# The planner's price of long scalar_tensor_tensor operations, raised from n/960 to n/760

## The chip, the cores and the metric

The kernel runs on one core of one Trainium2 chip. The time is the device time of one execution in microseconds; lower is better. Engines are named as in the profile: PE is TensorE's matrix multiply, PEld its weight loads, DVE is VectorE, ACT is ScalarE, POOL is GpSimd and SP is SyncE, which issues most of the DMAs.

## The reference

The reference is a two-layer encoder trunk on x of shape 1 x 512 x 1024 in float32. Each layer applies four sub-layers, every one with an RMS norm before and after it and a residual addition:

```python
for l in range(DEPTH):                         # DEPTH = 2
    h = swiglu(rms_norm(x, norm_pre[l, 0]), ffn1_gate[l], ffn1_up[l], ffn1_down[l])
    x = x + 0.5 * rms_norm(h, norm_post[l, 0])
    h = parallel_head_groups(rms_norm(x, norm_pre[l, 1]), ...)   # 4 retention heads, 4 gated DeltaNet heads
    x = x + rms_norm(h, norm_post[l, 1])
    h = memory_cross_attention(rms_norm(x, norm_pre[l, 2]), rms_norm(mem, mem_norm[l]), ...)
    x = x + rms_norm(h, norm_post[l, 2])
    h = swiglu(rms_norm(x, norm_pre[l, 3]), ffn2_gate[l], ffn2_up[l], ffn2_down[l])
    x = x + 0.5 * rms_norm(h, norm_post[l, 3])
```

Two lines of it matter here. The norm is `y = x * rsqrt(mean(x * x) + eps) * w`, and the gated DeltaNet group passes its 12 blocks of 128 columns (four heads each of q, k and v) through a centred depthwise convolution of five taps, followed by silu.

## The kernel before

**A planner orders the instructions.** The program is written as threads (Python generators) that yield one operation at a time. `Sched.run` keeps a clock for each engine, asks for each waiting operation when its operands are ready, and emits operations one after another. The emitted order is the order in which each engine executes; the chip then waits on semaphores where data is not there yet. The times of the planner are used for nothing else: a price changes no instruction, only who goes first.

An operation's length is what `cost` returns. When an operation reads what another wrote, the planner adds `SAME` (0.12 us, same engine) or `OTHER` (0.23 us, another engine). Among the operations that wait for an engine, the planner takes the one of the lowest priority number among those that can start no more than `WAIT` later than the earliest one:

```python
SAME, OTHER = 0.12, 0.23
WAIT = {"PE": 0.25, "ACT": 0.3, "DVE": 0.4, "POOL": 0.2, "SP": 0.0}
...
th = min((c for c in cands if c[0] <= t0 + WAIT[e]), key=lambda c: (pr(c[1]), c[0]))[1]
```

A thread shows its next operation only once its present one has been emitted.

**The work.** Every float32 matrix product is done as three products of rounded parts: an operand is split into a high part H (a copy on ACT) and a low part L (a subtraction on DVE), and `mm3` issues H·H, H·L and L·H. The weights come in blocks of 1 MB, named `raw`, loaded by SP into two buffers (`Stream.loader`), and are split by one thread, `Stream.cutter`, into `wts` tiles: an ACT copy and a DVE subtraction of 128x1024. The cutter's priority is 0, 1, 30 or 60, the higher the more split pieces lie ready. The thread `stream` (priority 50) issues the dense matmuls in a fixed order.

**Where the re-priced operations stand.** `stt` is the helper for `scalar_tensor_tensor`, (a op scalar) op b on DVE. Four places issue it on 256 elements or more:

- `chain`, one thread for each of the four row tiles t of x in every transition between sub-layers: twice (a half of 512 each) `x = hw * rsqrt + x`, and twice `tmp = x * rsqrt * wpre`. Between them stand sums of squares on ACT and a rsqrt of small operations, on POOL for most tiles and on DVE for tile 3 (`POST_DVE`, `PRE_DVE`). The priorities of the tiles are `PRIO = (-1, -1, 13, -1)`. Each `tmp` half starts a thread `feat`: four transposes on PE, a copy to uH on ACT, a subtraction to uL on DVE.
- `early.conv.one`: four in a row on `cv`, one for each tap beside the middle one, for each of 12 blocks in each layer.
- `prepare`: eight on `T` of 896 elements, background work in the first sub-layer.

Around a transition, `out_proj` issues the last products of a sub-layer, and `first_group` the first ones of the next: four column blocks on the first 256 rows (which needs the features of tiles 0 and 1), then the same on the other 256 (tiles 2 and 3). In the mixed sub-layer, `ret_head` loads T, q, k and v of a retention head by SP from DRAM, where `side` has put them, and multiplies k by q on PE (`ps<-q,k`); `inverse` and `scan` are the DeltaNet group's chains.

All instructions carry one line number, L235, since the planner's `emit` issues them all.

## Time and profile before

| | us |
|---|---|
| runs of the kernel (median; lowest to highest of 3) | 2445.86 (2445.59 to 2447.47) |
| the profiled execution: its own time | 2445.77 |
| its span, first to last instruction | 2444.0 |
| PE busy in the span | 2399.7 (98%) |
| DVE busy | 1686.7 (69%) |
| ACT busy | 1122.4 (46%) |
| POOL busy | 203.4 (8%) |

The profile is one execution of the program. Its stages are read by windows of time: a transition between sub-layers takes some 40 us of the span (365 to 405 is the first), the gated feed-forward sub-layers some 300, the mixed sub-layer some 300 (layer 0: 405 to 685; layer 1: 1610 to 1880). "Granted clock" (PEclk) is the share of full speed that TensorE was given in a stretch. A matmul's end is modelled, so its start is the safer number.

### The profile page before, as it was taken

The numbers are of one execution on the slowest core, as the hardware profiler recorded it, in microseconds if no ns is written. First come the engines' busy times: TensorE is split into PE (matmuls) and PEld (weight loads), VectorE is DVE, ScalarE is ACT, GpSimd is POOL, SyncE is SP. The second block draws the span as 40 slices with busy tenths as digits, with TensorE's granted clock in tenths as the row PEclk, the third lists the DMA queues.
The fourth block names the chain that finished last, engine by engine and source line by source line (L and its number), as shares of the span: only waits on it lengthen the run. The fifth ranks groups of instructions, "written<-read, shape, count | busy, mean of one in ns | idle before, by whom it ended". The sixth has DMA issues, their size and how long they took to land. (4 is left out here: it accounts for less than half of the span.)

```text
span 2444.0 us, 37654 instructions
## 1 busy us (share of the span) xinstructions
PE 2399.7 (98%) x15206; PEld 2128.4 (87%) x15206; DVE 1686.7 (69%) x2660; ACT 1122.4 (46%) x1886; POOL 203.4 (8%) x584
## 2 busy tenths in 40 slices
PE   8999999999999999999999999999999999999998
PEld 7889888886989889998889998888788898899987
DVE  5588637867776568886388885486877665788852
ACT  4524525742345544555245553366324454455631
POOL 1000001221020020001010000114010200100011
PEclk9999999999999999999999999999999999999999
DMA  6622522355334322334213334225553243133330
GB/s 204 202 95 82 177 86 96 99 175 159 99 121 153 109 86 70 114 108 176 86 35 104 106 120 160 81 93 145 163 153 132 89 164 104 35 104 104 127 141 35
DMA packets 231204, 286.83 MB, mean 117 GB/s; under 512 B 29630, under 2 KB 190966, under 8 KB 231030
## 3 DMA queue, kind: packets, MB, share of 16 engines
q1 hardware_dynamic: 229878, 280.23, 35.6%
q10 hardware_dynamic: 1152, 4.19, 0.4%
q8 instruction: 119, 1.95, 0.3%
q14 instruction: 55, 0.45, 0.1%
HBM read 255.00 MB, written 29.39 MB: 116 GB/s over the span
## 5 line engine op out<-in xcount | busy, mean ns | idle before, releaser
L235 PE MATMUL ps<-uH,wts 128*128 128x256 f32 (+1 forms) x4064 | 973.1, 325 | 2.5 <-ACT sg L235 2.0
L235 PEld LDWEIGHTS ps<-uH,wts 128*128 128x128 f32 x4064 | 690.3, 189 | 63.6 <-ACT sg L235 2.2
L235 PE MATMUL ps<-uL,wts 128*128 128x256 f32 (+1 forms) x2032 | 655.9, 323 | 0.6 <-DVE uL L235 0.6
L235 DVE TENSOR_TENSOR wts<-raw,wts 128x1024 fp32r<-128x1024 f32 (+1 forms) x363 | 408.5, 1134 | 141.9 <-ACT wts L235 139.3
L235 ACT ACTIVATE wts<-raw 128x1024 fp32r<-128x1024 f32 (+1 forms) x363 | 354.5, 983 | 202.8 <-PE ps L235 115.4
L235 PEld LDWEIGHTS ps<-uL,wts 128*128 128x128 f32 x2032 | 386.8, 190 | 30.8 <-DVE uL L235 1.5
L235 PE MATMUL ps<-wts,uH 128*128 128x512 f32 x1152 | 356.8, 391 | 0.0
L235 PEld LDWEIGHTS ps<-wts,uH 128*128 128x128 f32 x1152 | 214.9, 188 | 43.6
L235 PE MATMUL ps<-wts,uL 128*128 128x512 f32 x576 | 224.6, 390 | 0.0
L235 ACT ACTIVATE sg<-ps 128x256 f32<-128x256 f32 (+1 forms) x208 | 98.0, 473 | 273.1 <-PE ps L235 272.8
L235 DVE TENSOR_TENSOR wts<-T,wts 128x1024 fp32r<-128x1024 f32 x120 | 147.0, 1225 | 51.3 <-ACT wts L235 50.7
L235 ACT ACTIVATE wts<-T 128x1024 fp32r<-128x1024 f32 x120 | 126.9, 1057 | 62.8 <-DVE T L235 62.8
L235 PEld LDWEIGHTS ps<-wts,uL 128*128 128x128 f32 x576 | 108.2, 188 | 22.8
L235 DVE TENSOR_TENSOR uL<-h,uH 128x512 fp32r<-128x512 f32 x76 | 51.2, 689 | 107.5 <-ACT uH L235 107.4
L235 POOL TENSOR_SCALAR sm<-sm 128x1 f32<-128x1 f32 (+1 forms) x165 | 39.2, 238 | 836.8 <-ACT junk L235 812.1
L235 ACT ACTIVATE uH<-h 128x512 fp32r<-128x512 f32 x76 | 46.3, 626 | 132.0 <-PE ps L235 126.9
L235 ACT ACTIVATE junk<-ps 128x512 bf16<-128x512 f32 (+1 forms) x96 | 47.0, 490 | 113.6 <-PE ps L235 99.2
L235 POOL TENSOR_SCALAR wpost<-wpost 128x1024 f32<-128x1024 f32 x4 | 20.3, 5087 | 925.7 <-DMA wpost<-in_norm_post_dram 701.0
L235 PE MATMUL ps<-s3H,wts 128*128 128x256 f32 x480 | 94.6, 281 | 0.0
L235 PE MATMUL ps<-s2H,wts 128*128 128x256 f32 x480 | 94.6, 281 | 0.0
L235 PE MATMUL ps<-s1H,wts 128*128 128x256 f32 x480 | 94.6, 281 | 0.0
L235 DVE TENSOR_TENSOR sg<-ps,sg 128x512 f32<-128x512 f32 x120 | 79.9, 685 | 16.0 <-ACT sg L235 15.9
(340 smaller groups left out, 4324.4 us busy)
## 6 DMA issues: line engine op xcount, KB each, us to landing
raw<-in_ffn_up_dram SPq DMA_DIRECT2D x44, 1024.0 KB, 5.2
raw<-in_ffn_down_dram SPq DMA_DIRECT2D x44, 1024.0 KB, 4.9
raw<-in_ffn_gate_dram SPq DMA_DIRECT2D x43, 1024.0 KB, 5.2
raw<-in_w_in_dram SPq DMA_DIRECT2D x32, 1024.0 KB, 6.1
raw<-in_w_out_dram SPq DMA_DIRECT2D x8, 1024.0 KB, 5.7
raw<-in_xattn_q_dram SPq DMA_DIRECT2D x8, 1024.0 KB, 5.1
raw<-in_xattn_k_dram SPq DMA_DIRECT2D x8, 1024.0 KB, 5.0
raw<-in_xattn_v_dram SPq DMA_DIRECT2D x8, 1024.0 KB, 4.9
```

The source lines that it names most:

```text
L235: fn(*a, **kw)
```

## The change

In `cost`, DVE's `scalar_tensor_tensor` of 256 elements or more is priced with n/760 in place of n/960. For 512 elements in SBUF the price goes from 0.07 + 512/960 = 0.603 us to 0.07 + 512/760 = 0.744 us, for 896 from 1.003 to 1.249. No instruction is added, removed or altered; the planner may emit them in another order.

```diff
     if kind == "DVE":
         if name in ("tensor_copy", "tensor_scalar", "memset") and not psum:
             return 0.07 + n / 1920
-        return (0.13 if psum else 0.07) + n / 960
+        return (0.13 if psum else 0.07) + n / (760 if name == "scalar_tensor_tensor" and n >= 256 else 960)
```

## The prediction

> **What bounds the kernel now.** First the page's head: span and busy shares.

> ```profile
> span 2444.0 us, 37654 instructions
> PE 2399.7 (98%) x15206; PEld 2128.4 (87%) x15206; DVE 1686.7 (69%) x2660; ACT 1122.4 (46%) x1886; POOL 203.4 (8%) x584
> ```

> TensorE is the bound; the change touches no matmul. What an order can win or lose is PE's idle 2444.0 − 2399.7 = 44.3 us. The windows by stage say where that lies (columns: stretch, its length, busy time and count of PE, PEld, DVE, ACT, POOL, then granted clock, DMA share, GB/s).

> ```profile
> 0.00:20.00 20.00, 9.22 (x46) 8.36 (x47) 11.55 (x30) 10.88 (x16) 5.68 (x22) 1.00 0.73 239
> 20.00:365.00 345.00, 341.85 (x1840) 296.19 (x1838) 223.27 (x289) 137.20 (x172) 7.14 (x22) 1.00 0.42 136
> 365.00:405.00 40.00, 38.71 (x263) 34.91 (x262) 29.60 (x74) 19.80 (x42) 11.40 (x44) 1.00 0.29 99
> 405.00:520.00 115.00, 114.81 (x584) 94.01 (x583) 82.70 (x152) 78.05 (x157) 27.62 (x61) 1.00 0.43 122
> 520.00:685.00 165.00, 158.43 (x1184) 132.51 (x1183) 126.61 (x279) 61.05 (x134) 8.30 (x8) 0.98 0.43 138
> ...
> 1720.00:1880.00 160.00, 153.35 (x1161) 129.10 (x1161) 119.46 (x269) 54.09 (x124) 8.30 (x8) 0.97 0.42 129
> ...
> 2070.00:2110.00 40.00, 38.71 (x249) 34.25 (x248) 29.54 (x73) 17.44 (x39) 12.35 (x48) 1.00 0.07 20
> ...
> 2437.00:2444.00 7.00, 0.00 (x0) 0.00 (x0) 3.62 (x14) 0.69 (x2) 0.00 (x0) 0.61 0.28 105
> ```

> Start and end hold 10.8 + 7.0 us, the first sub-layer 3.2, the two retention stretches 6.6 + 6.6 and each of seven transitions about 1.3. The waits of PE name the releasers (total, times, longest).

> ```profile
> PE ps L235 <- DVE tmp L235: 17.1, 9, 8.5
> PE ps L235 <- DMA k<-qkd: 11.8, 2, 6.1
> ...
> PE ps L235 <- DVE uL L235: 1.9, 8, 0.6
> ```

> The 8.5 is the start, before any product. Of DVE's work only `tmp` and `uL` in the transitions keep PE waiting, 17.1 − 8.5 + 1.9 = 10.5 us in all.

> **The change, part by part.** The re-priced operations are these groups:

> ```profile
> L235 DVE SCALAR_TENSOR_TENSOR cv<-xp,cwT,cv 128x512 f32<-128x512 f32 x96 | 74.6, 788 | 11.3 <-ACT cv L235 9.0
> L235 DVE SCALAR_TENSOR_TENSOR x<-tmp,sm,x 128x512 f32<-128x512 f32 x64 | 45.8, 749 | 54.7 <-POOL sm L235 54.4
> L235 DVE SCALAR_TENSOR_TENSOR tmp<-x,sm,wpre 128x512 f32<-128x512 f32 x64 | 45.4, 750 | 7.7 <-POOL sm L235 6.3 <-DMA wpre<-in_norm_pre_dram 0.4 <-POOL sel L235 0.3
> L235 DVE SCALAR_TENSOR_TENSOR T<-crel,lg,T 128x896 f32<-128x896 f32 x8 | 9.2, 1150 | 0.2
> ```

> The plan counts (96 + 64 + 64) × 0.141 + 8 × 0.246 = 33.5 us more on its DVE clock; the chip's own durations stay. So the direct term is 0, and all turns on order.

> *Is the new price nearer?* A record of 0.75 us looks like 0.744. But a plan's price is the distance to the next operation, and its latency is price plus 0.12 or 0.23. The timeline has both:

> ```profile
> 2080.74 0.75 DVE L235 SCALAR_TENSOR_TENSOR x<-tmp,sm,x 128x512 f32<-128x512 f32 x1 [1.47 <-POOL sm L235]
> 2081.58 0.63 ACT L235 ACTIVATE junk<-x 128x512 bf16<-128x512 f32 x1 [0.90 <-DVE x L235]
> ...
> 2099.29 1.42 DVE L235 SCALAR_TENSOR_TENSOR tmp<-x,sm,wpre 128x512 f32<-128x512 f32 x2
> ```
> ```profile
> 430.95 3.10 DVE L235 SCALAR_TENSOR_TENSOR cv<-xp,cwT,cv 128x512 f32<-128x512 f32 x4
> ```

> Two independent ones take 1.42, so the second starts 1.42 − 0.75 = 0.67 after the first: the old price is 0.07 short, the new one 0.07 long. To ACT it is 2081.58 − 2080.74 = 0.84: the old plan says 0.603 + 0.23 = 0.83, the new 0.97. A tap that waits for the tap before starts (3.10 − 0.75) / 3 = 0.78 later: old 0.72, new 0.86. The error changes sign more than size, so I expect no general gain from a truer plan.

> [...]

> *Transitions (seven alike).* Rows of the last one before the final sub-layer's body:

> ```profile
> 2078.78 1.27 PE L235 MATMUL ps<-ident,tmp 128*128 128x128 f32 x8
> 2079.39 0.42 PEld L235 LDWEIGHTS ps<-ident,tmp 128*128 128x128 f32 x4 [0.25 <-issue]
> ...
> 2084.63 1.05 ACT L235 ACTIVATE wts<-raw 128x1024 fp32r<-128x1024 f32 x1
> ...
> 2089.03 0.75 DVE L235 SCALAR_TENSOR_TENSOR x<-tmp,sm,x 128x512 f32<-128x512 f32 x1 [1.14 <-POOL sm L235]
> 2089.69 1.28 DVE L235 TENSOR_TENSOR uL<-ps,uH 128x512 fp32r<-128x512 f32 x2
> ...
> 2090.43 0.19 PEld L235 LDWEIGHTS ps<-uL,wHx 128*128 128x128 f32 x1 [0.49 <-DVE uL L235]
> ...
> 2096.18 1.22 DVE L235 TENSOR_TENSOR wts<-raw,wts 128x1024 fp32r<-128x1024 f32 x1
> ...
> 2101.61 1.41 DVE L235 SCALAR_TENSOR_TENSOR tmp<-x,sm,wpre 128x512 f32<-128x512 f32 x2 [0.90 <-POOL sm L235]
> ...
> 2102.42 1.38 PE L235 MATMUL ps<-ident,tmp 128*128 128x128 f32 x8 [0.88 <-DVE tmp L235]
> ```

> (a) Tiles 0 and 1: eight transposes stand together, with 0.25 us lost between the fours, since the second `tmp` half is late. In the plan four transposes take 4 × 2 × 128/2400 = 0.43 and the second half comes 0.603 after the first: a wait of 0.18, under PE's allowance of 0.25, so the transposes stay together. With 0.744 the wait is 0.32, over it, unless PE came to the first four more than 0.07 late. Then a matmul group goes between and fills the hole. PE's steps are groups of about 0.64 in the plan, so the first four come up to 0.39 late; on time within 0.07 they are in about half of the 14 cases (0.32 of 0.64). Gain 7 × 0.2 = 1.4 us (the quarter, less what the later uH costs); ends 0 and 14 × 0.25 = 3.5.

> (b) The start of `first_group`: PE waits 0.49 for uL, which stands behind `x` of tile 2. The new price makes tiles 0 and 1 later in the plan, so uL stays behind `x`. I take 0. A loss is possible if something slips in ahead of uL (third rival); the best is the whole wait, 7 × 0.49 = 3.4.

> (c) The last `tmp`: PE idles 0.88 because DVE idles 0.90 for POOL's small operations, which are not re-priced. With the POOL chain unhurried the 7 × 0.88 = 6.2 us stay. The cover is gone if DVE's order ahead of that chain changes; tile 2's second `x` comes behind tile 3's chain, whose gaps (0.12 in the plan) are under DVE's allowance of 0.4 by either price, so I take 0.

> *The convolutions.* In 405 to 520 the plan's DVE gets 48 × 0.141 = 6.8 us heavier, against 115 − 82.7 = 32.3 free on the chip; PE is busy 114.8 of 115. The plan may hold the end of this stretch up to 6.8 later against PE. What hides it is that the following chains start from matmuls of the stream. 0 for the stretch itself.

> *Retention.* The largest single stalls are here:

> ```profile
> 555.65 0.38 SPq L235 DMA_DIRECT2D raw<-in_w_in_dram  x1
> 556.09 0.57 SPq L235 DMA_DIRECT2D q<-qkd  x1
> ...
> 563.30 6.04 PE L235 MATMUL ps<-q,k 128*128 128x512 f32 x8 [5.76 <-DMA k<-qkd]
> ```
> ```profile
> 583.02 3.59 PE L235 MATMUL ps<-q,k 128*128 128x512 f32 x8
> ```
> ```profile
> 556.00:566.00 10.00, 4.24 (x11) 2.12 (x10) 9.31 (x23) 4.23 (x5) 0.00 (x0) 0.76 0.65 195
> 566.00:576.00 10.00, 10.00 (x39) 7.10 (x38) 7.59 (x16) 1.06 (x1) 0.00 (x0) 0.90 0.57 180
> ```

> q's load is issued behind a 1 MB weight load; PE stands 5.76 us, the granted clock falls (0.76, then 0.90), and the eight products take 6.04 us where the next head's take 3.59: 5.76 + 2.45 = 8.2 us. Both layers do it (11.8 us in two waits), so the fault is in how the plan prices DMAs and the queue, not in an stt. I take 0; ends −8.2 (gone in one layer) and +5.4 (one more load of 1.05 MB ahead, at the window's 195 GB/s) a layer.

> [...]

> *The rest.* `T` in `prepare`, the initial `tmp` and the final `x` have no rival work whose place matters: 0, hidden by PE's 341.9 of 345 us in the first sub-layer; uncovered, 8 × 0.246 = 2 us.

> **Sum.** −1.4 against the profiled execution's 2445.77 gives 2444.4; the median of the runs is 0.09 above it, hence 2444.5 us.

> **Rivals.**
> 1. *A retention stall goes* (faster). If the re-planned end of the convolutions puts q ahead of the weight load in one layer: 2445.8 − 8.2 = 2437.6; in both 2429. For it: 6.8 us of shift in the plan just ahead. Against: both layers stall alike though they differ in surroundings.
> 2. *The new price is the true one.* Then the waits for `tmp` and `uL` shrink: 10.5 less the 6.2 that POOL makes, 2445.8 − 4.3 = 2441.5, still within 0.2%. Against it stands the 0.67.
> 3. *A weight split ahead of uL* (slower). A split's ACT copy is done from 2084.63 on, and its DVE half waits until 2096.18 for a plan gap over 0.4. The re-pricing makes uL later in the plan by 0.14 and more; where the gap behind tile 2's `x` passes 0.4, the 1.22 us split goes in at 2089.69, and PE waits 1.13 more (what the split holds DVE), seven times 7.9: 2444.4 + 7.9 = 2452.3. Against: in the present plan no gap there is wide enough, and tile 2's second `x`, of better priority than the split, may take the place for 0.67.
> 4. *A later q* (slower): one more load ahead, 2444.4 + 5.4 = 2449.8 for one layer, 2455.2 for both. It decides as soon as a split of the weights is emitted ahead of the rotary products in DVE's queue, since its end lets SP issue that load. For it: DVE is busy 9.31 of the 10 us in which PE stands, so the order there is tight. Against: no price in that stretch is changed.
> 5. *Nothing moves*: the order stays where it counts, 2445.9.

> **How the numbers follow.** About 0.2% (4.9 us) is what a measurement of this kernel can tell from no change. My forecast with 5 and 2 takes 0.52 (0.36, 0.08, 0.08), all "same"; rival 1 0.19, and small gains that add up past 4.9 us 0.02; rival 3 0.12; rival 4 0.15, the larger since a shift of up to 6.8 us in the plan can move q either way and the stall is already there. Faster 0.21, same 0.52, slower 0.27. The range runs from one stall gone, with a little more, 2436.5, to rival 4 in both layers, 2455. The likeliest case alone spans 2441 to 2448.

> **What would show it.** Right: PE busy again 98%; in the transitions some pairs of four transposes parted by dense products; the 0.88 us wait for the last `tmp` still seven times; PE's wait for `k<-qkd` still two of about 6 us. Wrong: that wait gone or above 8 us; a `wts` subtraction between `x` of tile 2 and uL with PE's wait for uL near 1.6; PE waiting behind `cv`; a new idle stretch where the mixed sub-layer's output projection starts, from the DeltaNet chain being emitted later.

## The result and the profile after

The change makes the kernel 0.8% slower: 2465.18 us (median of 4 runs, 2461.08 to 2470.85) against 2445.73 (4 runs, 2443.38 to 2447.47), a ratio of 1.0082 with a 95% interval of 1.0059 to 1.0105. The forecast was 2444.5 and the range ended at 2455. The profiled execution of the changed kernel is its lowest, 2461.08 us with a span of 2459.3, so the profile accounts for 15.3 us. The other three, 2463.21, 2467.15 and 2470.85, have mean granted clocks of 0.994, 0.992 and 0.992 against its 0.995; what such a clock costs is found below. One run each of two kernels below (2644 us, the price on the transitions alone; 2979 us, both together) had a mean granted clock of 0.85 and 0.75 and is left out of the ratios.

The head of the page after, and the windows by stage that answer to those of before (stretch, length, busy time and count of PE, PEld, DVE, ACT, POOL, granted clock, DMA share, GB/s):

```profile
span 2459.3 us, 37627 instructions
PE 2401.3 (98%) x15206; PEld 2127.7 (87%) x15206; DVE 1692.5 (69%) x2660; ACT 1123.2 (46%) x1888; POOL 203.8 (8%) x584
```
```profile
20.00:365.00 345.00, 341.02 (x1844) 295.09 (x1843) 223.85 (x291) 141.03 (x178) 7.78 (x23) 1.00 0.42 136
365.00:405.00 40.00, 38.24 (x268) 35.09 (x267) 30.48 (x73) 20.02 (x39) 11.20 (x43) 1.00 0.31 106
405.00:520.00 115.00, 106.44 (x529) 85.11 (x529) 78.02 (x143) 71.68 (x151) 28.28 (x61) 0.99 0.41 115
520.00:685.00 165.00, 162.33 (x1191) 136.64 (x1190) 126.36 (x280) 60.19 (x134) 9.20 (x8) 0.97 0.42 135
```

The convolution stretch, 405 to 520, had PE busy 114.81 of 115 us before and has it busy 106.44 after: 8.6 us of idle time where there was 0.2. The retention stretch has less idle time than before (2.7 us against 6.6). Nothing else moves much. A finer cut of the first stretch:

```profile
405.00:425.00 20.00, 18.38 (x90) 13.26 (x89) 11.87 (x41) 7.00 (x14) 0.00 (x0) 1.00 0.24 79
425.00:445.00 20.00, 17.45 (x88) 14.06 (x88) 18.82 (x33) 17.29 (x46) 4.27 (x3) 1.00 0.09 27
445.00:465.00 20.00, 20.00 (x100) 16.78 (x101) 16.96 (x21) 16.47 (x38) 1.99 (x1) 1.00 0.52 139
465.00:490.00 25.00, 20.61 (x103) 15.83 (x103) 19.75 (x38) 19.47 (x32) 6.24 (x16) 0.93 0.36 102
```

The waits of PE (total, times, longest) say what is late:

```profile
PE ps L235 <- ACT wts L235: 12.1, 7, 1.7
PE ps L235 <- DVE tmp L235: 11.6, 5, 8.6
PE ps L235 <- DVE gl L235: 9.1, 6, 2.5
PE ps L235 <- DMA k<-qkd: 5.4, 2, 2.9
PE ps L235 <- ACT kT L235: 3.0, 2, 1.5
```

`gl` and `kT` are new. They are operands of the key transposes and of the decay products, both in the convolution stretch. Three of these waits in the timeline (start, length, engine, operation, idle time before it and its releaser):

```profile
424.05 0.39 PE L235 MATMUL ps<-uH,wts 128*128 128x512 f32 x1
425.28 0.63 ACT L235 ACTIVATE kT<-cv 128x512 f32<-128x512 f32 x1
425.96 0.66 PE L235 MATMUL ps<-ident,kT 128*128 128x128 f32 x4 [1.52 <-ACT kT L235]
...
442.95 0.40 PE L235 MATMUL ps<-uH,wts 128*128 128x512 f32 x1
444.73 0.15 DVE L235 COPY gl<-ps 128x4 f32<-128x4 f32 x1
444.94 0.50 PE L235 MATMUL ps<-grow,sel 128*128 128x512 f32 x1 [1.59 <-DVE gl L235]
...
472.38 0.15 DVE L235 COPY gl<-ps 128x4 f32<-128x4 f32 x1
472.59 0.50 PE L235 MATMUL ps<-grow,sel 128*128 128x512 f32 x1 [2.53 <-DVE gl L235]
```

Read them so: the stream's dense matmul at 442.95 is followed by a decay product whose operand DVE writes only at 444.73. PE idles for 1.59 us, and whatever comes later in the planner's order, dense matmuls of the stream among it, starts behind that product.

**Two stretches of each layer.** Three landmarks are easy to find: the first `ps<-ident,tmp` transpose of the transition into the mixed sub-layer (370.10 us before, 368.59 after), the first `ps<-q,k` product (563.30, 569.76) and the first product of the output projection, `ps<-wts,hsH` (675.29, 683.96). The differences of these starts are the first stretch (transposes to q k, with the convolutions) and the second (q k to output projection, with the DeltaNet inverse). In us, layer 0 / layer 1:

| | first stretch | second stretch | all the rest |
|---|---|---|---|
| before | 193.2 / 193.6 | 112.0 / 112.0 | 1833.2 |
| after | 201.2 / 202.6 | 114.2 / 111.0 | 1830.3 |

So 8.0 + 9.0 us are lost in the first stretches, 1.2 in the second ones, and 2.9 are gained elsewhere: 15.3. The rest scatters between 1828 and 1837 us over the kernels below (n/700 apart, which has 1843), so little can be read from its 2.9.

### The profile page after: what moved, and what is told of

It is laid out like the page before. It is cut to its first block, busy times and chain, and to the rows that moved or that the text cites. A ratio compares the mean times of both kernels' runs of the same rounds, so it can differ in the third digit from the quotient of the medians.

```text
span 2459.3 us, 37627 instructions
## 1 busy us (share of the span) xinstructions
PE 2401.3 (98%) x15206; PEld 2127.7 (87%) x15206; DVE 1692.5 (69%) x2660; ACT 1123.2 (46%) x1888; POOL 203.8 (8%) x584
## 5 line engine op out<-in xcount | busy, mean ns | idle before, releaser
L235 PE MATMUL ps<-uH,wts 128*128 128x256 f32 (+1 forms) x4064 | 973.1, 324 | 2.9 <-ACT sg L235 2.0
L235 PEld LDWEIGHTS ps<-uH,wts 128*128 128x128 f32 x4064 | 689.5, 188 | 64.3 <-ACT sg L235 2.2
L235 PE MATMUL ps<-uL,wts 128*128 128x256 f32 (+1 forms) x2032 | 655.0, 322 | 0.2
L235 DVE TENSOR_TENSOR wts<-raw,wts 128x1024 fp32r<-128x1024 f32 (+1 forms) x363 | 408.6, 1132 | 164.2 <-ACT wts L235 151.7
L235 ACT ACTIVATE wts<-raw 128x1024 fp32r<-128x1024 f32 (+1 forms) x363 | 355.1, 983 | 213.4 <-PE ps L235 140.1
L235 PEld LDWEIGHTS ps<-uL,wts 128*128 128x128 f32 x2032 | 386.3, 190 | 31.2 <-issue 1.9
L235 PE MATMUL ps<-wts,uH 128*128 128x512 f32 x1152 | 360.0, 394 | 0.0
L235 PEld LDWEIGHTS ps<-wts,uH 128*128 128x128 f32 x1152 | 215.4, 189 | 43.0
L235 PE MATMUL ps<-wts,uL 128*128 128x512 f32 x576 | 225.1, 391 | 0.0
L235 ACT ACTIVATE sg<-ps 128x256 f32<-128x256 f32 (+1 forms) x208 | 98.0, 473 | 268.9 <-PE ps L235 268.7
L235 DVE TENSOR_TENSOR wts<-T,wts 128x1024 fp32r<-128x1024 f32 x120 | 147.0, 1225 | 49.5 <-ACT wts L235 48.6
L235 ACT ACTIVATE wts<-T 128x1024 fp32r<-128x1024 f32 x120 | 126.9, 1058 | 66.6 <-DVE T L235 66.6
L235 PEld LDWEIGHTS ps<-wts,uL 128*128 128x128 f32 x576 | 108.7, 189 | 22.9
L235 DVE TENSOR_TENSOR uL<-h,uH 128x512 fp32r<-128x512 f32 x76 | 51.4, 691 | 103.8 <-ACT uH L235 103.8
L235 POOL TENSOR_SCALAR sm<-sm 128x1 f32<-128x1 f32 (+1 forms) x165 | 39.2, 238 | 851.9 <-ACT junk L235 826.9
L235 ACT ACTIVATE uH<-h 128x512 fp32r<-128x512 f32 x76 | 46.2, 626 | 126.9 <-PE ps L235 122.6
L235 ACT ACTIVATE junk<-ps 128x512 bf16<-128x512 f32 (+1 forms) x96 | 47.2, 491 | 120.4 <-PE ps L235 106.2
L235 POOL TENSOR_SCALAR wpost<-wpost 128x1024 f32<-128x1024 f32 x4 | 19.4, 4854 | 928.6 <-DMA wpost<-in_norm_post_dram 703.4
L235 PE MATMUL ps<-s1H,wts 128*128 128x256 f32 x480 | 94.0, 280 | 0.0
L235 PE MATMUL ps<-s2H,wts 128*128 128x256 f32 x480 | 94.0, 280 | 0.0
L235 PE MATMUL ps<-s3H,wts 128*128 128x256 f32 x480 | 94.0, 280 | 0.0
L235 DVE TENSOR_TENSOR wLx<-raw,wHx 128x1024 fp32r<-128x1024 f32 x45 | 54.3, 1222 | 51.2 <-ACT wHx L235 51.2
```

The lines of the kernel that those rows point to most:

```text
L235: fn(*a, **kw)
```

## The experiments

Two theories stood at the beginning. In the plan as well as in the trace, the changed kernel lets the eight matmuls of the gates go ahead of the convolution's one transpose (`cw`) at the start of the mixed sub-layer, where the kernel before has them the other way about. *Theory A*: this swap is the loss. *Theory B*: the higher price of the convolution's four products spoils the order of the convolution stretch.

### Swap and price, one at a time

Four kernels make a square. The first gives the changed kernel the old place of the transpose, by a priority:

```diff
-        work = [(self.gates(l, ep, ring), 6, "gates"), (conv(), 7, "conv"), ...
+        work = [(self.gates(l, ep, ring), 6, "gates"), (conv(), 5.5, "conv"), ...
```

> The changed kernel, with the convolution thread's priority 5.5 in place of 7, so that its one transpose of the tap weights goes ahead of the eight gate matmuls at the start of the mixed sub-layer, as it does in the kernel before. Theory A (the loss is that order: the gate matmuls go first and the convolutions start late): the PE waits for kT, kqv and gl in the 40 us behind it go and some 8 us a layer come back, 2446 to 2451 us, with what the transitions lost (0.8 us in two of them) left over. Theory B (the convolutions' higher price makes the order inside the stretch worse, wherever it starts): no more than a third comes back, 2459 us or more.

Measured: 2462.4 us (2458.21 to 2465.61), ratio to the kernel before 1.0070 (1.0056 to 1.0085).

The second gives the kernel before, at the old price, the new place: the transpose waits for the gates' matmuls.

```diff
         def conv():
             cw = self.early_in[0]
+            yield self.has("abmm")
```

> The kernel before, old price, with one line that holds the convolution thread until the eight gate matmuls are emitted. Theory A: it pays the loss without any new price, 5 to 9 us a layer, 2456 to 2464 us. Theory B: the price is not touched, so 2446 us within 4.

Measured: 2436.19 us (2431.83 to 2444.12), ratio 0.9968 (0.9956 to 0.9981). Faster than the kernel before.

The third and fourth split the price by place: on the convolution's products alone, and on the transition's `x` and `tmp` alone.

```diff
-    ... name == "scalar_tensor_tensor" and n >= 256 else 960)
+    ... name == "scalar_tensor_tensor" and n >= 256 and out.tensor.name.startswith("cv") else 960)
```

> The new price for the convolutions' operations on cv alone, the old one for x, tmp and T. In the planner's own order the convolution transpose stays ahead of the gates. Theory A: 2446 us within 4. Theory B: most of the loss is here, 2458 us or more.

Measured: 2470.15 us (2462.72 to 2474.73), ratio 1.0100 (1.0083 to 1.0117).

```diff
+    ... name == "scalar_tensor_tensor" and n >= 256 and not out.tensor.name.startswith(("cv", "T_")) else 960)
```

> The new price for x and tmp in the transitions alone, the old one for cv and T. The planner puts the gates ahead of the convolution transpose in both layers. Theory A: most of the loss, 2456 to 2466 us. Theory B: 2446 to 2449 us, the transitions' own part alone.

Measured: 2436.8 us (median), ratio 0.9965 (0.9953 to 0.9978).

| us | transpose first | gates first |
|---|---|---|
| old price on `cv` | 2445.7 (before) | 2436.2 (second), 2436.8 (fourth) |
| new price on `cv` | 2470.2 (third), 2462.4 (first) | 2465.2 (the change) |

At the old price on `cv`, gates first is a gain of 9 us, so theory A, by which that order is the loss, is refuted. Theory B is right on the price of `cv`, which costs 17 to 24 us in the left column and 28 to 29 in the right, but had not seen the gain. Both parts are in the change: its price on the transitions turns the swap, and its price on the convolutions loses. They do not simply add, since at the new price on `cv` the swap gains nothing (2462.4 us without it, 2465.2 with it). Undoing the swap there did bring the first stretches back, from 201.2 and 202.6 us to 192.6 and 192.1, much as theory A expected; but the second ones grew from 114.2 and 111.0 to 121.9 and 120.3. One loss was traded for another, and the two sections on the stretches below take them one at a time. The price on `T` was not tried alone.

Why the transition's price turns the swap can be read from the planner's own times (us of the plan, at the start of the mixed sub-layer of layer 0):

```text
              PE free   operands of the gates' matmuls ready   goes first
before        383.69    384.72                                 conv transpose (ready long before)
after         387.15    387.00                                 gates (lower priority number, and ready)
```

With dearer chains the plan's transition ends later on PE than on DVE, and the choice falls the other way: PE is free 1.03 us ahead of the gates' operands before, and 0.15 us behind them after. Why it gains shows at the first q k products of the second kernel:

```profile
561.71 0.30 PEld L235 LDWEIGHTS ps<-q,k 128*128 128x128 f32 x2 [1.79 <-DMA q<-qkd]
561.74 3.67 PE L235 MATMUL ps<-q,k 128*128 128x512 f32 x8 [1.40 <-DMA k<-qkd]
```

Before, PE stood 5.76 us here and then took 6.04 for the eight products. Now it stands 1.40 and takes 3.67: it comes later, since the swap costs it some waits on the way, q and k come 1.6 earlier, and behind the shorter wait the granted clock stays at 1.00 (556 to 566 and 566 to 576; 0.76 and 0.90 before).

### Is it the price, and does its size matter?

The expectations from here on speak of *theory C*: the price only brings about orders, and the loss is made of stalls at places where the plan thinks TensorE idle (the first stretch) and of the DeltaNet inverse left without dense products beside it (the second). *Theory D* is in each case the plainest rival.

Three kernels have one price at every place, below and above that of the change.

```diff
-        return (0.13 if psum else 0.07) + n / (760 if name == "scalar_tensor_tensor" and n >= 256 else 960)
+        return (0.13 if psum else 0.07) + n / (800 if name == "scalar_tensor_tensor" and n >= 256 else 960)
```

> The price n/800 at every place (the change has n/760, the kernel before n/960). In this plan the gates' products go ahead of the convolution's transpose, as after the change; the plan's idle time of TensorE in the first 100 us of the mixed sub-layer is 3.5 us (0.4 before, 3.0 with the gates held first under the old price, 9.5 after the change), and the order of retention against inverse is that of before. Theory C: the loss is made of two things that a plan has or has not, stalls where the plan thinks TensorE idle, and the inverse left without dense products beside it; neither grows with the price. So the time is near that of the gates-first kernels, 2434 to 2441 us. Theory D: the price itself is the harm, and it grows with it: three quarters of the way from 2436 to 2465 us, 2452 to 2462 us.

Measured with n/800: 2440.06 us (2437.89 to 2444.21), ratio 0.9978 (0.9968 to 0.9989).

> The price n/700 at every place, a higher one than the change has. In this plan the gates' products go first, TensorE's planned idle time in the first 100 us of the mixed sub-layer is 5.8 us, and the products of head 1 stand ahead of the inverse with two of the stream's groups between. Theory C: 2436 us, and per layer 2 to 3 us for the larger planned idle time, less what the wait for q and k gives back: 2437 to 2447 us, faster than the change in spite of the higher price. Theory D: the price is the harm: 1.4 times the loss, 2470 to 2485 us.

Measured with n/700: 2450.57 us (2447.11 to 2455.18), ratio 1.0020 (1.0010 to 1.0030). A miss for theory C too, by 3.6 us: the mixed sub-layers kept within it (first stretches 192.2 and 193.4, second 109.6 and 109.5), but "all the rest" is 1843.4, 10 more than before. Three of its transitions account for that: PE waits there for `tmp` for 2.2, 1.9 and 2.2 us (up to 731, 901 and 1938), and behind these waits the granted clock is at half for 6.8, 3.4 and 6.8 us. Half of their sum is 8.5 us.

> The price n/868 at every place: 0.66 us for 512 elements, which is the spacing that the trace shows (0.67 us from one such operation to the next). In this plan the convolution's transpose goes first, as before; the planned idle time of TensorE in the first 100 us of the mixed sub-layer is 4.4 us, of which 3.9 us stand ahead of one decay product; the order of retention against inverse is that of before. Theory C: 4 us more of stalls per layer at that product, and as TensorE then comes later to the products q k, the wait there (5.9 us, with 6.8 us of half clock behind) gives most of it or more back: 2438 to 2450 us. Theory D, the price is the harm: 0.4 of the loss of 24 us, 2453 to 2458 us. Theory E, a truer price makes a better plan: below 2440 us.

Measured with n/868: 2440.28 us (2433.12 to 2443.5), ratio 0.9974 (0.9964 to 0.9985).

The loss doesn't grow with the price: n/800, most of the way to n/760, is faster than before, and n/700 is slower by a quarter of what n/760 loses. The price that the trace would choose, n/868, does no better than n/800 or than the old price with the swap, so nothing here shows that the truer plan is the better one.

### The first stretch: idle time that only the plan has

The planner's PE clock has holes, where no operation was ready in the plan. In the first 100 us of the mixed sub-layer, counted from its first product, there are 0.4 us of them before and 9.5 after. At each of the larger ones in after's plan the stream holds all four of its banks and waits for one, presumably since the plan has the convolutions slower, and the planner puts into the hole whatever becomes ready next. The chip may have no such hole, or have it elsewhere; PE comes early to that operation and stands. In after's plan the holes are 1.0 us ahead of the gates' transposes, 2.1 ahead of a `kT` transpose, 2.2 ahead of a value transpose, 1.9 and 1.1 ahead of decay products. The trace has waits at these operations: 0.5, 1.5, 0.5, 2.5 and 0.8 us. The wait of 1.6 us at 444.94 has no hole of its own.

To try it, a third buffer for the convolutions' results gives the plan its way out:

```diff
-        ring, cvs = self.ring(ep, "kqv", [S], 6), self.ring(ep, "cv", [S], 2)
+        ring, cvs = self.ring(ep, "kqv", [S], 6), self.ring(ep, "cv", [S], 3)
```

> The changed kernel with a third buffer for the convolutions' results (two before). In this plan TensorE's planned idle time in the first 100 us of the mixed sub-layer falls from 9.5 to 2.7 us, gates first as after the change; but all of the stream's free groups are planned ahead of the products of head 1, so that the inverse has none beside it. From the first transpose of the second transition to the first q k product the change takes 201.2 and 202.6 us in the two layers, against 193.2 and 193.6 before; from there to the output projection 114.2 and 111.0 us, against 112.0 and 112.0. Theory C (the stalls are planned idle time that the chip does not have, filled by products whose operands are late): the first stretch falls to 191 to 195 us in each layer; the second may grow to 117 to 127 us if the half clock settles on the inverse. Time 2446 to 2472 us by that, the first stretch being the test. Theory D (the stalls come of DVE or of the gates' place): the first stretch stays at 199 us or more.

Measured: 2460.29 us (2458.12 to 2462.22), ratio 1.0070 (1.0057 to 1.0082). First stretches 193.9 and 193.0 us, second 119.1 and 121.9: both as theory C has it.

The control, the same buffer at the old price with the gates first:

> The control of the third buffer: the old price, the gates held first (2436.2 us with two buffers), and three buffers for the convolutions' results. Planned idle time 3.5 us (3.0 with two buffers), order of retention against inverse as before. Theory C: a buffer more is worth nothing by itself; first stretch 191 to 193 us (191.1 and 191.3 with two), time 2433 to 2440 us. If the third buffer helps the chip by itself, whatever the plan: below 2430 us, and what the changed kernel gains by it says nothing of the plan.

Measured: 2443.73 us (2440.18 to 2452.11), ratio 1.0004 (0.9994 to 1.0013). Another miss: the buffer costs 7 to 9 us there, with stalls of 8.3 us at holes of 3.5. But it answers what it was for: a third buffer is no help by itself, so what it did in the changed kernel came through the plan.

All kernels side by side, for layer 0. "Stalls" is what the starts of successive matmuls are apart beyond the usual spacing (0.227 us for 512 columns, 0.118 for 256, 0.111 for 128), summed from 30 to 120 us behind the first transpose; "q k" is the same sum for the one gap ahead of the first q k product; the last column is the first stretch less both.

| kernel | plan's holes | stalls | q k | first stretch | less both |
|---|---|---|---|---|---|
| before | 0.4 | 3.9 | 5.9 | 193.2 | 183.4 |
| new price on `cv` alone | 0.4 | 2.7 | 8.3 | 195.1 | 184.1 |
| change, transpose first | 2.1 | 3.4 | 5.4 | 192.6 | 183.8 |
| change, third buffer | 2.7 | 3.9 | 5.9 | 193.9 | 184.1 |
| old price, gates first | 3.0 | 6.1 | 1.6 | 191.1 | 183.4 |
| price on the transitions alone | 3.0 | 6.0 | 1.4 | 191.2 | 183.8 |
| n/800 | 3.5 | 5.7 | 0.0 | 191.0 | 185.3 |
| old price, gates first, third buffer | 3.5 | 8.3 | 0.8 | 194.2 | 185.1 |
| n/868 | 4.4 | 7.0 | 0.7 | 191.0 | 183.3 |
| n/700 | 5.8 | 6.8 | 0.9 | 192.2 | 184.5 |
| the change | 9.5 | 14.9 | 2.7 | 201.2 | 183.5 |

Kernels with more holes in the plan have more stalls, though not one for one. Up to the 5.8 us of n/700 the first stretch lies between 191.0 and 195.1 us, on either side of before's 193.2, since the stalls come out of the wait for q and k, which is there anyway. In the change that wait no longer covers them: 9.1 us more of holes than before, 11.0 more of stalls, and 3.2 back from the wait for q and k. Of these stalls 1.7 us are the half clock of 3.4 us behind the wait at 472.59; in layer 1 a half clock of 6.8 us behind the same wait makes 3.4 of the 9.0 us. That holes beyond what the wait covers are paid in full is thus seen in one kernel only; that they are the cause rests on the third buffer and on the transpose put first, each of which took them out of the plan and the stalls out of the trace.

### The second stretch: the clock on small products

The kernel with the new price on `cv` alone has hardly a stall in the first stretch and still loses 15.2 and 10.2 us, in the second (127.2 and 122.2 against 112.0). Its windows there:

```profile
586.00:592.00 6.00, 5.83 (x72) 3.22 (x70) 4.85 (x11) 2.35 (x8) 0.00 (x0) 1.00 0.75 287
592.00:602.00 10.00, 8.67 (x148) 8.15 (x149) 6.26 (x12) 1.69 (x3) 1.03 (x1) 0.50 0.30 99
602.00:612.00 10.00, 10.00 (x91) 9.42 (x90) 3.22 (x4) 1.77 (x3) 6.32 (x6) 0.50 0.01 3
612.00:623.00 11.00, 11.00 (x99) 10.32 (x98) 4.33 (x8) 0.00 (x0) 1.83 (x2) 0.51 0.02 5
```

PE is busy and the granted clock is 0.50, for 30.7 us by the trace's clock records. Before, 592 to 602 and 602 to 612 had 1.00. These are the DeltaNet inverse's products of 32x32 and 64x64. In this plan the stream's last free groups went ahead of retention head 1, and the inverse stands alone, with two waits:

```profile
590.63 1.19 PE L235 MATMUL ps<-X,Tb 32*32 32x32 f32 x32
...
592.56 1.91 PE L235 MATMUL ps<-Tb,Am 32*32 32x32 f32 x32 [0.73 <-ACT Ta L235]
```

Two experiments on this kernel. One adds work: a product over all 128 rows ahead of each group of small ones, in a part of the bank that nothing reads.

```diff
+        def dense(op, out):
+            more = self.mm(out[:, 0:128], self.uH[:, 0, 0:64].bitcast(F32), self.uH[:, 0, 0:128].bitcast(F32))
+            op.calls = more.calls + op.calls
+            return op
...
-                yield join(*[self.mm(px[pb, i], Am[pa, 16 * d + i, pb], ...
+                yield dense(join(*[self.mm(px[pb, i], Am[pa, 16 * d + i, pb], ...), other)
```

> This is the kernel with the new price on the convolution's products alone (2470.2 us), its instructions in the same order, with one product of full depth (128 rows, 64 columns, 128 elements, single precision, about 0.21 us of TensorE's time at the full clock) put ahead of each group of small products of the DeltaNet inverse: 24 per layer, about 5 us of work more per layer. They write a part of the bank that nothing reads, and the planner does not see them. Theory C: the 15 us that this kernel loses per layer between its first products q k and the state's products are the half clock of 30.7 us, and the clock stays at half because the products of 32x32 and 64x64 standing alone do not count as enough work; with the dense products between them the half clock at 592 us shrinks to 10 us or less, and the time falls in spite of the added work, to 2446 to 2462 us. Theory D: the clock is a follower of the waits or of the order, and the added work only adds: 2480 to 2495 us, half clock of 30 us or more at 592 us.

Measured: 2500.55 us (2499.34 to 2502.63), ratio 1.0225 (1.0212 to 1.0238), half clocks of 23.9 and 44.4 us. Theory C missed: one such product in each group did not hold the clock up. Theory D's 2495 us was passed too. Each product took 0.36 us at the full clock (589.42 to the next start at 589.78), not the 0.21 of the expectation, an estimate: a quarter of a q k product of 512 columns, two records 0.429 us apart in the kernel before, makes as much; the second stretches less half of their time at half clock are 121.0 and 119.7 us, 20.6 more in all than without the products, and the longer half clock costs 9.7. The place at which the half clock of layer 0 ends tells more:

```profile
615.73 0.69 PE L235 MATMUL ps<-uH 128*64 128x128 f32 x2
616.35 1.06 PE L235 MATMUL ps<-X,Ta 32*32 32x32 f32 x16
617.33 3.63 PE L235 MATMUL ps<-v,oT 128*128 128x128 f32 x16
620.89 0.43 PE L235 MATMUL ps<-uH 128*64 128x128 f32 x2
```

The pair of 0.69 us is 0.43 again behind 3.6 us of full 128x128 products in one piece, the first piece of that length in this stretch. The length alone does not decide it: in the kernel without the added products a piece as long left the clock at half, which came back only at 622.7. How the two lay on the grid of the clock's changes stands at the end of this text.

```profile
606.85 3.78 PE L235 MATMUL ps<-v,oT 128*128 128x128 f32 x16
```

The other adds nothing and moves four groups of the stream to where PE waits:

```diff
             for k in range(KD):
+                if nm == "z0" and k == 4:
+                    yield self.has("sc10", "sc11", "sc12", "sc13")
```

> The kernel with the new price on the convolution's products alone (2470.2 us), with the stream held at the middle of one of its stripes until the four products of head 1 have been placed: four of its groups, 12 matmuls of 128x512, so come between the first groups of small products of the DeltaNet inverse, where the trace has two waits of 0.9 us, instead of ahead of them. No work is added. Theory C: the half clock of 30.7 us in the first layer and 17.1 us in the second, which costs most of the 15 and 10 us that this kernel needs more from q k to the output projection (127.2 and 122.2 us against 112.0), starts at those waits; with dense products in them it shrinks to 10 us or less, that stretch falls to 111 to 118 us, and the time to 2447 to 2460 us. Theory D (the stretch is long for another reason, the small products or late operands): it stays at 120 us or more, and the time at 2466 to 2475 us.

Measured: 2459.72 us (2451.94 to 2462.24), ratio 1.0064 (1.0052 to 1.0077); second stretches 117.4 and 117.5. The place was right, 10.4 us. The mechanism that the expectation gave, waits that bring the clock down, was not:

```profile
588.00:598.00 10.00, 10.00 (x188) 7.97 (x187) 8.64 (x19) 2.98 (x9) 1.04 (x1) 0.99 0.59 220
598.00:608.00 10.00, 10.00 (x113) 9.54 (x111) 5.36 (x7) 2.83 (x5) 3.59 (x4) 0.50 0.30 102
```
```profile
594.36 0.39 PE L235 MATMUL ps<-uH,wts 128*128 128x512 f32 x1
594.68 1.10 PE L235 MATMUL ps<-Tb,Am 32*32 32x32 f32 x29
...
595.71 1.08 PE L235 MATMUL ps<-Ta,Am 32*32 32x32 f32 x29
596.64 1.10 PE L235 MATMUL ps<-X,Ta 32*32 32x32 f32 x29
...
597.67 1.46 PE L235 MATMUL ps<-Tb,Am 32*32 32x32 f32 x26
```

PE does not wait any more, 10.00 of 10.00 us by the profile, and at 597.8 the clock halves all the same, 3.1 us into a run of 32x32 products without a dense one, for 10.2 us instead of 30.7. The kernel before has dense `v,oT` products at 597.53 in the middle of that run.

The price of it is the same in every kernel. The second stretch, and the time at half clock within it (layer 0 / layer 1):

| kernel | second stretch | at half clock | stretch less half of it |
|---|---|---|---|
| old price, gates first | 109.3 / 108.9 | 0 / 0 | 109.3 / 108.9 |
| before | 112.0 / 112.0 | 4.8 / 6.6 | 109.6 / 108.7 |
| the change | 114.2 / 111.0 | 9.8 / 3.4 | 109.3 / 109.3 |
| `cv` alone, groups moved | 117.4 / 117.5 | 14.5 / 14.9 | 110.2 / 110.0 |
| change, third buffer | 119.0 / 121.9 | 20.7 / 25.8 | 108.7 / 109.0 |
| change, transpose first | 121.9 / 120.3 | 22.8 / 18.1 | 110.5 / 111.3 |
| `cv` alone | 127.2 / 122.2 | 35.4 / 23.2 | 109.5 / 110.6 |

Over all the kernels without added work the last column stays between 107.8 and 111.3, while the first moves by 18 us. The orders of the second stretch are worth next to nothing in themselves; what they cost is the clock.

### Both together

> The changed kernel with both: the third buffer for the convolutions' results (2460.3 us alone: first stretch 193.9 and 193.0 us, second 119.1 and 121.9) and the hold of four of the stream's groups until the products of head 1 are placed. The plan puts two of them between those products and the transposes behind, where the trace has TensorE waiting 2.9 us, and two more beside the first small products of the inverse. Theory C, both places: the first stretch stays at 191 to 195 us, the half clock behind 590 us (17.1 and 20.5 us without the hold) shrinks to 10 us or less, the second stretch falls to 111 to 117 us in both layers, and the time to 2446 to 2455 us, within 0.4% of the kernel before at the diff's own price. Theory D, the price costs something beside those two places: the stretches as said, the time still at 2458 us or more; or the second stretch stays at 118 us or more, and the hold does not work on this order.

Measured: 2453.81 us (median), ratio 1.0032 (1.0020 to 1.0045). First stretches 193.4 and 193.2, second 115.9 and 118.5 (14.3 and 18.9 us at half clock), the rest 1832.3. The time is within what theory C gave, layer 1's second stretch is 1.5 beyond it, and the half clock behind 590 us shrank to 10.2 and 13.7 us, from 17.1 and 20.5, where 10 or less was expected. Of the 19.5 us that the change lost, 11.8 are back with the price untouched. What is left, 7.7, lies in the second stretches, which are 3.9 and 6.5 over before in the profiled execution; less half of their time at half clock they are 108.8 and 109.0.

The best of these kernels is the one with the old price and the gates held first, 2436.19 us: 0.3% faster than before, 1.2% than the change. The price on the transitions alone gets the same, by the same swap.

## Why the prediction was wrong, point by point

- *The direct term, 0*: right. The four products on `cv` in a row take 3.17 us after (at 422.55) and took 3.10.
- *The new price is no truer than the old*: as far as the runs go, right. n/868, between them, is 5.6 us faster than the kernel before, but so are a worse price, n/800, and the old price with the swap.
- *Transitions (a)*: the mechanism was right, and more often than thought: in all seven the transposes of tiles 0 and 1 stand in fours with three matmuls between, not in about half of the 14 cases.

```profile
2095.12 0.60 PE L235 MATMUL ps<-ident,tmp 128*128 128x128 f32 x4
2096.25 0.60 PE L235 MATMUL ps<-ident,tmp 128*128 128x128 f32 x4
```

- *Transitions (b)*: better than the likeliest case. PE's waits for `uL` fell from 1.9 us in eight to 0.5 in one.
- *Transitions (c)*: wrong. The second half of the last `tmp` is emitted behind two `uL` subtractions, and PE waits 1.73 us, put down to `wts`, where it waited 0.88. That gives back what (a) and (b) gained; from the second transition to the fifth the distance to the kernel before stays between 8.2 and 8.6 us.

```profile
2118.72 1.48 DVE L235 TENSOR_TENSOR uL<-ps,uH 128x512 fp32r<-128x512 f32 x2 [0.56 <-ACT uH L235]
2120.11 0.74 DVE L235 SCALAR_TENSOR_TENSOR tmp<-x,sm,wpre 128x512 f32<-128x512 f32 x1
2121.00 0.63 PE L235 MATMUL ps<-ident,tmp 128*128 128x128 f32 x4 [1.73 <-ACT wts L235]
```

- *The convolutions, 0*: this is the step that failed. "What hides it is that the following chains start from matmuls of the stream." The 6.8 us of plan time were counted rightly, and so was the free time of DVE on the chip, 32.3 us. But the question was what the plan does with its own PE clock: in the plan the stream itself stands, for want of banks, and other products are emitted into 9.5 us of holes. The term, put at 0, measured 17 us: 8.0 and 9.0 in the two layers, 1.7 and 3.4 of them by the half clock behind one of the waits. The page showed nothing of this, since the chip has no such holes; it stands only in the planner's times.
- *Retention, 0, with −8.2 to +5.4 a layer*: the likeliest case failed, the ends held. The wait did move: q's load is issued 5.4 us later (561.50 against 556.09), but PE comes later still, waits 2.54 us and loses less clock (half of it for 3.4 us from 569.35, where it was 6.8 from 561.24). This is rival 1's gain reached from the other side: not an earlier q, a later PE. What a shorter stall at this place cost differs: behind 1.40 us (old price, gates first) nothing was lost and the eight products took 3.67 us; behind the 2.54 us there was still a half clock of 3.4 us.
- *What none of the rivals had*: the swap at the start of the mixed sub-layer, and the clock of the inverse. Rival 3 (a weight split ahead of uL) did not happen; rival 4 had the right sign for a wrong reason.

## What to carry to other kernels

Where a planner's price changes, read the plan's own idle time on the engine that bounds the kernel, before and after: a hole that only the plan has can be filled with work that the chip then waits for. The size of a price tells little of the size of its effect, since an order flips as soon as one start passes another; before a price is judged, flip that order by hand at the old price, as that may be the gain. And look at the granted clock where the matmuls are small: with the new price on `cv` alone PE was busy 10.00 of 10.00 us from 602 to 612 at a clock of 0.50, and full-size products moved in there, by the order alone, gave back 10.4 us.
